# Order of the output stages' halves, and of some sums, loads and weights, in a two-layer encoder kernel

## Chip, core and metric

The kernel runs on one core of a Trainium2 chip. The time is the device time of one execution in microseconds; the time before is a median of 3 runs.

## What is computed

A trunk of two layers over 1024 tokens of 1024 features, with 256 memory tokens, all in float32. Cut from the reference:

```python
for l in range(DEPTH):                                  # 2 layers
    h = rmsnorm(x, norm_gain[l])
    mk, mv = jnp.split(memn @ w_mem_kv[l], 2, axis=-1)
    if l % 2 == 0:
        qa, ka, va, qb, kb, vb, qm, gate = split_cols(h @ w_in_even[e], SPLIT_EVEN)
        # qa, ka: per-head rmsnorm and 2-D rope; ya: global attention, 8 heads
        # yb: window of +-128 tokens with a sink and a bias, 8 heads; ym: attention to memory
        y = jnp.concatenate([ya, yb, ym], axis=-1) * jax.nn.silu(gate)
        x = x + y @ w_out_even[e]
    else:
        qc, kc, vc, qm, gate = split_cols(h @ w_in_odd[o], SPLIT_ODD)
        # yc: attention to 8 x 16 neighbours on the token grid, 16 heads; ym: memory
        y = jnp.concatenate([yc, ym], axis=-1) * jax.nn.silu(gate)
        x = x + y @ w_out_odd[o]
return rmsnorm(x, final_norm_gain)
```

## The kernel before, in words

Every product is taken in three parts for precision: a float32 operand is split into a high part (rounded, `wh`, `H`, `t`) and the rest (`wl`), and TensorE (PE) multiplies high by high, high by low and low by high. ACT makes high parts (L122), DVE or POOL low parts (L155, L1250, L126). Weights come through four buffers: a raw tile `wraw` by SP's DMA queue (L135 in `wload`, L1295 in `out_project`), then `wh` and `wl`. PE's tiles are 128 x 512 in PSUM; `tr`, `sa`, `pv`, `pj`, `x`, `y` and `s` are PSUM tiles by their tags.

The program runs through these stages; the times are of the profiled execution.

- **prep** (to about 120 us) and the entry of **l0**: `project_a` computes norms, values, and keys and queries with rope (its last instruction is the sum `rp`, L869, on POOL) and the keys and values of the memory. `self.loaded` holds back weight loads in `wload` until a given instruction is issued.
- **l0** (to about 650 us): `even` runs global attention in pairs of heads, memory attention, and the windowed attention `window_pair`. Each result is multiplied with its gate by `gated_rows` (L505 to L520: sums on DVE and POOL and stores to DRAM arrays `y_k`). In l0 the weights are split on POOL, both `wh` (L153) and `wl` (L155).
- **out0** (about 645 to 780 us): `out_project`, the output product, by Strassen's scheme in Winograd's form on 2 x 2 blocks: seven products, each over four tiles (banks) of 6 x 128 rows, with weight sums `s1` to `s4` in DRAM made earlier. `y_parts` loads and splits the moving operand of a product (named t1, t2, t3, y22, y21, t4 there; the tile tags in PSUM order are `sa`, `tr`, `pv`, and the SBUF tags are q, k, va, v, H). `weights(i, kind)` loads and splits one bank's weights as two halves of 384 columns, u = 0 and 1. In the trace these are L1302 (matmuls) and L1250, L122 (splits). `plus` adds a bank to its sum (L1311).
- **front** (about 780 to 1035 us): products of layer 1's projection, again by seven products, in an order written out by hand in the string PLAN: `x` and `z` are products (12 matmuls each, L1549), `V` is a step of the values (L410, whose weights `t` are split on ACT and DVE, L402), `.` is a step of the norm, and a digit is that many steps of the operands' differences.
- **l1** (from about 1035 us): `odd` runs memory attention and the neighbourhood attention `near`; PE's order is pinned there to the written order. `near_bias`, `load_q` and `load_v` load what `near` needs; `values_of_two` stores values to `vd` (L421).
- **out1** (from about 1384 us): `out_project` again, with `self.held` a list of instructions that splits must stand behind.

What sets the order elsewhere is a scheduler with priorities: `ahead(kind)` moves an instruction forward by a number of places, and `issue_after(i)` forbids it to stand ahead of `i`. On its own engine and queue every instruction then runs in the order written.

## Time and profile before

| | |
|---|---|
| median of 3 runs | 1504.66 us (1504.38 to 1507.83) |
| the profiled execution's own time | 1509.32 us |
| its span, and clock granted to PE | 1507.5 us, 0.995 |
| PE busy | 1476.3 us (98%) |
| DVE, ACT, POOL busy | 1040.6, 839.5, 635.0 us |
| DMA | 271.90 MB, mean 180 GB/s |

The profile's page gives for each engine the busy time and the number of instructions. Of the 31.2 us in which PE is idle, 1.3 lie at the start, 6.4 behind the last matmul, and 22.4 in gaps of over 0.15 us between. A row such as `PE sa L1302 <- ACT wh L122: 1.8, 1, 1.8` says that PE waited for 1.8 us in all, once, at most 1.8 us, ahead of a matmul of line 1302 into the tile `sa`, and that the wait ended with ACT's instruction of line 122 that wrote `wh`. In a timeline a row starts with start and length in us, and a wait stands at its end in square brackets. In a chain of waits, each piece is what released the next.

### The profile page before, as it was taken

To read this page: it belongs to the slowest core of one execution; us is meant where nothing else is said; L and a number is where in the kernel's file an instruction comes from. 1 tells how busy PE (TensorE), PEld (TensorE's weight loads), DVE (VectorE), ACT (ScalarE), POOL (GpSimd) and SP (SyncE) were. 2 spreads that over 40 slices of the span, in tenths; PEclk is the share of its full clock that TensorE was granted. 3 is DMA by queue.
4 is the path that set the end of the run, shared out by engine and by line. 5 is a ranking of instruction groups with operands and counts; after the bars stand their busy time and mean duration, and the time that the engine had idled before them with its cause. 6 is when DMAs were issued, how large, how long until landed. Compare 5 with 4: busy or idle time off the path is not lost.

```text
span 1507.5 us, 25294 instructions
## 1 busy us (share of the span) xinstructions
PE 1476.3 (98%) x8377; PEld 1269.2 (84%) x8377; DVE 1040.6 (69%) x2121; ACT 839.5 (56%) x1855; POOL 635.0 (42%) x762
## 2 busy tenths in 40 slices
PE   9999999999999999999999999999999999999997
PEld 8897888989888788877879877888988888888886
DVE  5787777677676677677577776654347778788754
ACT  7733665655655456554444444444446777777443
POOL 1224567556765656443440000002325555654355
PEclk9999999999999999999999999999999999999998
DMA  8966244433333424387653343567864677688834
GB/s 286 319 159 185 93 125 165 126 120 123 128 126 135 136 87 138 114 283 257 195 179 106 125 138 135 160 168 256 289 192 158 191 242 218 215 288 308 294 113 138
DMA packets 173859, 271.90 MB, mean 180 GB/s; under 512 B 15648, under 2 KB 96800, under 8 KB 172704
## 3 DMA queue, kind: packets, MB, share of 16 engines
q1 hardware_dynamic: 173296, 270.20, 55.5%
q8 instruction: 66, 1.08, 0.3%
q14 instruction: 65, 0.53, 0.1%
q10 hardware_dynamic: 432, 0.09, 0.0%
HBM read 174.28 MB, written 83.89 MB: 171 GB/s over the span
## 4 chain that ended last, share of the span: by engine, by line
PE 47%; DVE 4%; DMA 3%; issue 1%; POOL 1%; ACT 1%; POOLq 0%; SPq 0%; DVEq 0%; ACTq 0%
PE pj L62 10%; PE x L1549 6%; PE pj L1302 4%; PE sa L1302 4%; PE pv L62 3%; PE y L1549 3%; PE s L62 3%; PE s L1302 3%; PE tr L1302 2%; PE tr L62 2%; PE pv L1549 2%; PE pv L1302 2%; PE pv L410 2%; PE y L410 1%; DMA v<-vt 1%
## 5 line engine op out<-in xcount | busy, mean ns | idle before, releaser
L122 ACT ACTIVATE ph<-tr 128x512 fp32r<-128x512 f32 (+2 forms) x336 | 180.5, 539 | 120.5 <-PE tr L130 79.7
L533 DVE TENSOR_TENSOR pl<-tr,ph 128x512 fp32r<-128x512 f32 (+2 forms) x336 | 205.5, 615 | 52.4 <-ACT ph L122 49.3
L237 PE MATMUL pj<-H,wh 128*128 128x512 f32 x704 | 234.7, 413 | 0.5 <-DVE vt L308 0.2
L153 POOL TENSOR_SCALAR wh<-wraw 128x512 fp32r<-128x512 f32 x48 | 32.0, 666 | 283.6 <-PE x L1549 240.4
L122 ACT ACTIVATE wh<-wraw 128x384 fp32r<-128x384 f32 (+1 forms) x163 | 89.0, 554 | 99.1 <-PE sa L1302 13.5
L237 PE MATMUL pj<-H,wl 128*128 128x512 f32 x352 | 138.9, 395 | 0.0
L237 PEld LDWEIGHTS pj<-H,wh 128*128 128x128 f32 x704 | 119.9, 189 | 18.5 <-POOL wl L155 0.6
L62 PE MATMUL pj<-H,wh 128*128 128x512 f32 x384 | 121.5, 397 | 0.0
L130 PE MATMUL tr<-ident,P 128*128 128x128 f32 x752 | 116.8, 273 | 2.5 <-POOL P L708 1.1
L1101 POOL TENSOR_SCALAR pn<-pn,st 128x384 f32<-128x384 f32 (+1 forms) x128 | 74.9, 586 | 101.3 <-DVE st L1100 64.1
L1250 POOL TENSOR_TENSOR wl<-wraw,wh 128x384 fp32r<-128x384 f32 x56 | 62.7, 1120 | 115.2 <-ACT wh L122 81.5
L130 PEld LDWEIGHTS tr<-ident,P 128*128 128x128 f32 x752 | 89.0, 140 | 12.2 <-DVE pl L533 2.7
L1099 ACT ACTIVATE pn<-pn,st 128x384 f32<-128x384 f32 (+1 forms) x128 | 75.1, 587 | 36.3 <-DVE st L1096 33.9
L1022 ACT ACTIVATE P<-sa,st 128x1024 f32<-128x1024 f32 x64 | 71.5, 1117 | 41.2 <-DVE st L1021 21.6
L1024 POOL TENSOR_SCALAR P<-P,st 128x1024 f32<-128x1024 f32 x64 | 74.1, 1161 | 32.4 <-DVE st L1023 32.4
L62 PE MATMUL s<-k,q 128*128 128x384 f32 (+1 forms) x352 | 86.3, 341 | 0.0
L1021 DVE TENSOR_REDUCE st<-sa 128x1 f32<-128x1024 f32 x64 | 77.6, 1218 | 10.8 <-PE sa L1017 9.2
L237 PEld LDWEIGHTS pj<-H,wl 128*128 128x128 f32 x352 | 66.2, 188 | 15.1
L62 PE MATMUL pj<-H,wl 128*128 128x512 f32 x192 | 75.8, 395 | 0.0
L155 POOL TENSOR_TENSOR wl<-wraw,wh 128x512 fp32r<-128x512 f32 x52 | 68.5, 1318 | 10.2 <-ACT wh L122 7.1
L1250 DVE TENSOR_TENSOR wl<-wraw,wh 128x384 fp32r<-128x384 f32 (+1 forms) x67 | 50.1, 747 | 31.3 <-ACT wh L122 31.0
L62 PEld LDWEIGHTS pj<-H,wh 128*128 128x128 f32 x384 | 66.7, 189 | 5.5
(506 smaller groups left out, 4207.9 us busy)
## 6 DMA issues: line engine op xcount, KB each, us to landing
wraw<-w_o SPq DMA_DIRECT2D x52, 256.0 KB, 3.9
y<-yb SPq DMA_DIRECT2D x24, 512.0 KB, 3.3
wraw<-s SPq DMA_DIRECT2D x64, 192.0 KB, 3.2
wraw<-w_e SPq DMA_DIRECT2D x44, 256.0 KB, 3.2
k<-k SPq DMA_DIRECT2D x42, 256.0 KB, 4.4
s<-bias SPq DMA_DIRECT2D x56, 192.0 KB, 2.0
y<-sg SPq DMA_DIRECT2D x20, 512.0 KB, 3.7
wq<-w_o SPq DMA_DIRECT2D x40, 256.0 KB, 3.6
```

The costliest lines, as they stand in the source:

```text
L62: return lambda *a, **k: self.tc.keep_in_program_order(getattr(self.engine, name)(*a, **k))
L122: return self.nc.scalar.activation(out, in_, AF.Copy, scale=scale)
L130: self.turned = self.fence = self.pe.transpose(o, i, self.ident)
L237: self.pe.matmul(a[:, :n], s[:, kt % UNIT, :], m, start=(kt == 0 and i == 0), stop=(kt == KT - 1 and i == 2))
L533: self.low = nc.vector.tensor_tensor(pl[:, :n], tr[:, :n], ph[:, :n], op=OP.subtract)
L1021: nc.vector.tensor_reduce(st[:, 0:1], s, axis=AX.X, op=OP.max, negate=True)
L1024: self.normal = nc.gpsimd.tensor_scalar(pt, pt, st[:, 2:3], 0.5, op0=OP.mult, op1=OP.mult)
L1099: nc.scalar.activation(o, o, AF.Exp, bias=st[:, 0:1], scale=-1.0, accum_out=st[:, 2:3])
L1101: normal = nc.gpsimd.tensor_scalar(o, o, st[:, 3:4], 0.5, op0=OP.mult, op1=OP.mult)
L1250: engine.tensor_tensor(lf, raw, hf, op=OP.subtract)
L1302: last = nc.tensor.matmul(bank, s[:, k, :], y[3 * u + k][m][:, cols], start=start and u + k + e == 0, stop=u == 1 and k + e == 4, skip_gro ...
L1549: self.last = nc.tensor.matmul(bank, ws[s][:, k, :], b[k][m], start=start and k + i == 0, stop=k == UNIT - 1 and i == 2, skip_group_check= ...
```

## The change

- PLAN: the third `x` product stands ahead of the first `V`.
- `project_a`: the loads of the memory's tokens for their norms, and weight loads behind them, stand behind the tenth weight load instead of behind the last transposition of the memory.
- `wparts`: where POOL makes `wh`, it stands behind the last rope sum.
- `even`: the gated rows of tile 6 are made step by step, one step per pair of blocks of the last window, behind POOL's last scaling there (`later_job`).
- `out_project`: the second and third product run over all four banks with the first half of their depth, then over all four with the second half (`products`), and the first two weights of the second product are loaded ahead of its moving operand.
- `behind_held`: in out1 the first sums, and at the end of `near` the last gated rows, stand behind `self.held`.
- `near_bias`, `load_q`, `load_v`: these loads stand behind the last store of values.

```diff
-PLAN = "x.x.V1V1V2V1V1V1V2V1V1V1V2V1V1V1V2V1x2z2V1V1V2V1V1V1V2V1V1V1V2V1V1V1V2V1x2z2z2z2"
+PLAN = "x.xx.V1V1V2V1V1V1V2V1V1V1V2V1V1V1V2V1x2z2V1V1V2V1V1V1V2V1V1V1V2V1V1V1V2V1z4z2z2"
...
             d = self.nc.sync.dma_start(raw, src)
+        self.raws.append(d)
...
-            nc.gpsimd.tensor_scalar(hf, raw, 1.0, 1.0, op0=OP.mult, op1=OP.mult)
+            with self.tc.issue_after(self.rotated.ins):
+                nc.gpsimd.tensor_scalar(hf, raw, 1.0, 1.0, op0=OP.mult, op1=OP.mult)
...
-                    nc.sync.dma_start(vd[:, :, b + e, :].rearrange("j p n -> p j n"),
+                    self.stored = nc.sync.dma_start(vd[:, :, b + e, :].rearrange("j p n -> p j n"),
...
             for t in range(0, len(todo), 2):
+                self.later_job(normal)
...
-        nc.gpsimd.tensor_tensor(rp, t1, u, op=OP.add)
+        self.rotated = nc.gpsimd.tensor_tensor(rp, t1, u, op=OP.add)
...
         vm = self.st("xv", [128, 2])
+        self.loaded = self.raws[9]
         self.rstd(io["mt"], [0, 1], vm, self.rs_m)
...
-        self.nc.sync.dma_start(bm, self.io["offsets"][h])
+        with self.tc.issue_after(self.stored.ins):
+            self.nc.sync.dma_start(bm, self.io["offsets"][h])
...
-        while self.later_jobs:
-            deque(self.later_jobs.popleft(), 0)
+        with self.behind_held():
+            while self.later_jobs:
+                deque(self.later_jobs.popleft(), 0)
...
+    def behind_held(self):
+
+        with ExitStack() as held:
+            for i in self.held:
+                held.enter_context(self.tc.issue_after(i.ins))
+            yield
...
-        def weights(i, kind):
+        def weights(i, kind, us=(0, 1)):
...
-            for c in cut:
+            for c in (cut[u] for u in us):
...
+        def products(y, banks, kind, start, ready=()):
+            ready = deque(ready)
+            for u in range(2):
+                for i, bank in enumerate(banks):
+                    (h, l), = (ready.popleft(),) if ready else weights(i, kind, (u,))
+                    for k in range(3):
+                        for e, (s, m) in enumerate(((h, 0), (h, 1), (l, 0))):
+                            nc.tensor.matmul(bank, s[:, k, :], y[3 * u + k][m], start=start and u + k + e == 0,
+                                             stop=u == 1 and k + e == 4, skip_group_check=True)
+                    if u:
+                        yield i
...
-            with self.ahead("sink"):
+            with self.behind_held(), self.ahead("sink"):
                 plus(at(c11, i), xb[i])
...
+        ready = [w for i in range(2) for w in weights(i, "s1", (0,))]
         y = self.y_parts(yd, tags["y"][1], "t1")
-        for i in range(4):
-            product(y, yb[i], weights(i, "s1"), True)
+        for i in products(y, yb, "s1", True, ready):
...
         y = self.y_parts(yd, tags["y"][2], "t2")
-        for i in range(4):
-            product(y, xb[i], weights(i, "s2"), False)
+        for i in products(y, xb, "s2", False):
...
-                self.lazily(lambda: self.gate(w, E_G + 6), lambda sg: self.gated_rows(sg, 6, y6, yd))
+                self.later_jobs = deque()
+                self.lazily(lambda: self.gate(w, E_G + 6),
+                            lambda sg: self.later_jobs.append(self.gated_steps(sg, y6, yd, ROWS.index(6))))
...
+        while self.later_jobs:
+            deque(self.later_jobs.popleft(), 0)
         self.gated_rows(sgs[0], 7, y, yd)
...
+    def later_job(self, normal):
+
+        if self.later_jobs:
+            with self.tc.issue_after(normal.ins):
+                if next(self.later_jobs[0], self) is self:
+                    self.later_jobs.popleft()
...
         def load_q(j):
-            return [self.load("q", qd[O_Q + j][i]) for i in range(2)]
+            with tc.issue_after(self.stored.ins):
+                return [self.load("q", qd[O_Q + j][i]) for i in range(2)]
...
         def load_v(j):
-            return self.load("v", vd[j // 2][j % 2], (128, 8, 256)).rearrange("p b (h d) -> p b h d", h=2)
+            with tc.issue_after(self.stored.ins):
+                v = self.load("v", vd[j // 2][j % 2], (128, 8, 256))
+            return v.rearrange("p b (h d) -> p b h d", h=2)
```

What this moves is seen in the order of the instructions on an engine. First POOL at the entry of l0 (about 130 to 148 us): `rp` is the last sum of a rope step, `wh` and `wl` the parts of the first gate weights, `P` the scaling of the first softmax. Before:

```order
L869 TENSOR_TENSOR rp_1734<-rt_323_1716,rt_328_1730 128x512
L153 TENSOR_SCALAR wh_2138<-wraw_2136 128x512
L155 TENSOR_TENSOR wl_2139<-wraw_2136,wh_2138 128x512
L869 TENSOR_TENSOR rp_1926<-rt_364_1908,rt_369_1922 128x512
L153 TENSOR_SCALAR wh_2144<-wraw_2142 128x512
L155 TENSOR_TENSOR wl_2145<-wraw_2142,wh_2144 128x512
L869 TENSOR_TENSOR rp_2008<-rt_375_1990,rt_380_2004 128x512
L153 TENSOR_SCALAR wh_2417<-wraw_2415 128x512
L155 TENSOR_TENSOR wl_2418<-wraw_2415,wh_2417 128x512
```

Now, the same piece:

```order
L874 TENSOR_TENSOR rp_1734<-rt_323_1716,rt_328_1730 128x512
L874 TENSOR_TENSOR rp_1926<-rt_364_1908,rt_369_1922 128x512
L874 TENSOR_TENSOR rp_2008<-rt_375_1990,rt_380_2004 128x512
L157 TENSOR_SCALAR wh_2138<-wraw_2136 128x512
L157 TENSOR_SCALAR wh_2144<-wraw_2142 128x512
L159 TENSOR_TENSOR wl_2139<-wraw_2136,wh_2138 128x512
L159 TENSOR_TENSOR wl_2145<-wraw_2142,wh_2144 128x512
L157 TENSOR_SCALAR wh_2417<-wraw_2415 128x512
L157 TENSOR_SCALAR wh_2423<-wraw_2421 128x512
L159 TENSOR_TENSOR wl_2418<-wraw_2415,wh_2417 128x512
```

All weights stand behind the last `rp`, and two `wh` ahead of two `wl`.

Second ACT at the entry of out0 (about 664 to 680 us): `wh` are the halves of the weights, `ph` and `bt` belong to the last attention, `q`, `k` and `va` are parts of the operand y22 of the fifth product (`y_parts`), loaded ahead. Before:

```order
L122 ACTIVATE wh_8263<-wraw_8261 128x384
L122 ACTIVATE ph_8120<-tr_8117 128x256
L122 ACTIVATE wh_8278<-wraw_8276 128x384
L122 ACTIVATE wh_8295<-wraw_8293 128x384
L122 ACTIVATE q_8708<-q_8708 128x512
L122 ACTIVATE wh_8310<-wraw_8308 128x384
L122 ACTIVATE q_8709<-q_8709 128x512
L122 ACTIVATE k_8710<-k_8710 128x512
L122 ACTIVATE wh_8327<-wraw_8325 128x384
```

Now:

```order
L124 ACTIVATE wh_8241<-wraw_8239 128x384
L124 ACTIVATE wh_8247<-wraw_8245 128x384
L124 ACTIVATE ph_8121<-tr_8118 128x256
L124 ACTIVATE wh_8294<-wraw_8292 128x384
L124 ACTIVATE wh_8309<-wraw_8307 128x384
L124 ACTIVATE q_8709<-q_8709 128x512
L124 ACTIVATE bt_8127<-pv_8041 64x512
L124 ACTIVATE q_8710<-q_8710 128x512
L124 ACTIVATE k_8711<-k_8711 128x512
L124 ACTIVATE k_8712<-k_8712 128x512
L124 ACTIVATE wh_8324<-wraw_8322 128x384
```

The four first halves of the second product (wh_8241, wh_8247, wh_8294, wh_8309) stand ahead of the first `q`; before, a `wh` stood behind each of the first `q` and `k`.

Third SP's queue at the entry of front (about 774 to 783 us): `wraw` of 128x512 are weights of the x products, those of 128x2x256 the weights `t` of the values, `wq` the operands of the weights' own sums. Before:

```order
L135 DMA wraw_9392<-w_o 128x512
L135 DMA wraw_9413<-w_o 128x2x256
L1767 DMA x_6_115<-yb_8151 128x512
L135 DMA wraw_9417<-w_o 128x2x256
L1767 DMA x_7_116<-yb_8151 128x512
L1588 DMA wq_9319<-w_o 128x512
```

Now:

```order
L137 DMA wraw_9393<-w_o 128x512
L137 DMA wraw_9412<-w_o 128x512
L1792 DMA x_6_115<-yb_8152 128x512
L137 DMA wraw_9433<-w_o 128x2x256
L1792 DMA x_7_116<-yb_8152 128x512
L1613 DMA wq_9320<-w_o 128x512
```

One more weight of an x product is ahead of the `wq` loads, and one load of `t` less. On PE the 12 matmuls of the third x product now stand between those of the second and the transpositions of `rq_y` (`tr` L130, now L132) ahead of the first matmul of the values.

More of the change, by code (lines that the diff above doesn't have):

```diff
@@ L84, in __init__ @@
         self.pe, self.ready, self.due = self.nc.tensor, {}, 0
-        self.loaded = None
+        self.loaded = self.rotated = None
+        self.raws = []
+        self.later_jobs = ()
     def ahead(self, kind):
@@ L420, in values_of_two @@
                     self.vec.tensor_tensor(o[:, :, :, 1, :], src, o[:, :, :, 0, :], op=OP.subtract)
-                    nc.sync.dma_start(vd[:, :, b + e, :].rearrange("j p n -> p j n"),
-                                      o.bitcast(F32).rearrange("p j h e d -> p j (h e d)"))
+                    self.stored = nc.sync.dma_start(vd[:, :, b + e, :].rearrange("j p n -> p j n"),
+                                                    o.bitcast(F32).rearrange("p j h e d -> p j (h e d)"))
             yield 3072
@@ L1191, in halves @@
         return tiles
+    @contextmanager
+    def behind_held(self):
[3 more added lines that the diff above has]
+            yield
     def y_parts(self, yd, tags, kind):
@@ L1207, in y_parts @@
                 nc.sync.dma_start(raw, src[kind])
-                with ExitStack() as held:
-                    for i in self.held:
-                        held.enter_context(self.tc.issue_after(i.ins))
+                with self.behind_held():
                     self.split(hi, lo, raw)
```

## Prediction

> **What bounds the kernel now.** I read the page's first part first, then what TensorE (PE) waits for, then the 25-us stretches around each wait, then the chain of waits there.
>
> ```profile
> PE 1476.3 (98%) x8377; PEld 1269.2 (84%) x8377; DVE 1040.6 (69%) x2121; ACT 839.5 (56%) x1855; POOL 635.0 (42%) x762
> ```
>
> PE is busy for 1476.3 us of a span of 1507.5 us, and no other engine passes 69%. In the order of its instructions PE has the same matmuls before and after the change, so the change can only move the 31.2 us in which PE stands, and what the clock costs. The list of PE's waits (us in total, times, longest) names where it stands:
>
> ```profile
> PE pv L62 <- DVE pl L533: 4.1, 8, 1.1
> ...
> PE sa L1302 <- ACT wh L122: 1.8, 1, 1.8
> PE y L410 <- ACT t L122: 1.6, 1, 1.6
> PE tr L130 <- POOL rp L869: 1.4, 2, 1.1
> ...
> PE tr L130 <- POOL P L708: 1.1, 3, 0.7
> ...
> PE tr L552 <- ACT wh L122: 1.1, 2, 0.7
> ...
> PE sa L1016 <- DVE q L126: 0.8, 1, 0.8
> ```
>
> All these groups but the first consist of one to three waits, so each is a place, not a habit of a loop; each part of the change lies at one of them. Then the stretches: start:end, length, busy us of PE, PEld, DVE, ACT, POOL, granted clock, DMA share, GB/s.
>
> ```profile
> 25.00:50.00 25.00, 23.44 (x167) 21.20 (x167) 12.07 (x25) 19.45 (x46) 9.03 (x7) 1.00 0.94 315
> 675.00:700.00 25.00, 23.13 (x92) 18.39 (x93) 16.00 (x23) 11.25 (x21) 10.39 (x9) 0.93 0.74 242
> 775.00:800.00 25.00, 21.71 (x120) 18.58 (x121) 15.83 (x33) 13.49 (x25) 5.84 (x4) 0.93 0.70 232
> ```
>
> Two stretches have a clock of 0.93, and both hold a wait: each loses about 0.07 x 25 = 1.7 us of full clock on top of the idle time. The Trainium skill, "TensorE: Matmul & The Clock Gate" (What's actually happening), has the clock halve after an idle window of about 3.4 us; the longest wait here is 1.8 us, so by that rule the two drops would not be there, and the trace disagrees with it in two places. By the rule the clock term below would be nothing, and the sum 1.7 us smaller in size.
>
> **The change part by part.** I sum against the profiled execution, 1509.32 us: its span of 1507.5 and 1.8 around it. It is 4.66 us above the median of 1504.66; I take differences over to the median. Signs: minus is time gained.
>
> *Loads of prep (raws[9]).* SP's issues, start and length:
>
> ```profile
> 24.91 2.99 SPq L785 DMA_DIRECT2D xt<-mt x3
> 28.26 1.68 SPq L135 DMA_DIRECT2D wraw<-w_mem x3
> ```
>
> The three mt loads and their 2.99 us stand ahead of weights for which PE waits (tr L552 behind wh, 1.1, and small ones after it, 1.56 us in all by PE's rows at 34.8 to 38.6). Now two of the weights go ahead of the mt loads. The queue is 0.94 busy there, so bytes only change places: what comes later are mt and w_a, whose users stand later in PE's order by 1.4 us. I take -1.0; ends -1.6 (all waits gone) and +2 (the mt loads, 2.99 us, late in their turn by two thirds).
>
> *POOL's weight splits behind the last rope sum.* POOL, then DVE, in the last two rope steps:
>
> ```profile
> 133.34 1.34 POOL L155 TENSOR_TENSOR wl<-wraw,wh 128x512 fp32r<-128x512 f32 x1
> ...
> 140.92 1.26 POOL L869 TENSOR_TENSOR rp<-rt,rt 128x512 f32<-128x512 f32 x1 [2.56 <-DVE rt L866]
> ...
> 147.65 1.12 POOL L1024 TENSOR_SCALAR P<-P,st 128x1024 f32<-128x1024 f32 x1 [1.55 <-DVE st L1023]
> ```
>
> ```profile
> 132.68 2.28 DVE L866 TENSOR_TENSOR rt<-rqn,c_sinq 128x256 f32<-128x256 f32 x2
> ...
> 137.13 1.25 DVE L766 SCALAR_TENSOR_TENSOR iq_t<-iq_t,rss 128x8 f32<-128x8 f32 x1
> ...
> 140.02 0.75 DVE L866 TENSOR_TENSOR rt<-rqn,c_sinq 128x256 f32<-128x256 f32 x2
> ```
>
> PE waits 1.09 us for the second rp and 0.76 us for q behind it. The same pair of DVE instructions takes 2.28 us beside POOL's wl and 0.75 us without it: 1.5 us of the chain to rp, and L766, with 8 columns, takes 1.25 us beside the next wl, about 1 too much. Without these, the last rp is there near 138, not at 142.2, and the first wait is gone; the second needs a split on DVE that also stands behind ACT, so I count 0.4 of its 0.76. Sum -1.5. What is late next: four wh and four wl (4 x 0.62 by POOL's rows and 4 x 1.3, together 7.7 us) now run after rp, to about 147, ahead of P, which starts at 147.65: cover of 0.6 us. Ends: -1.9 (both waits gone), +1 (rp not earlier, P pushed by about 2, half of it seen by PE).
>
> *Second product by halves, two weights ahead (out0).* The chain of waits, start and length:
>
> ```profile
> 668.81 6.00 DMA q<-y
> ...
> 674.83 0.63 ACT q L122
> ...
> 675.98 0.51 ACT wh L122
> ```
>
> ACT has the split of q (part of the operand y22 of the fifth product, loaded from y, 6.00 us) ahead of the weight wh that PE needs next, so the weight waits for a transfer that it has nothing to do with: 1.8 + 0.33 us of PE, and the clock drop right after. In the changed order all four first-half weights stand ahead of q, and PE has 36 matmuls (8.4 us) of first halves to do before any second half. Both waits go, -2.1, and with them the drop, -1.7. Earlier, tr waits 0.73 behind POOL:
>
> ```profile
> 645.57 3.07 POOL L708 TENSOR_SCALAR P<-P,st 128x384 f32<-128x384 f32 x4
> ```
>
> That P is queued behind three sums of gate 6 (L516, L517, L519, 4.3 us by POOL's rows from 641.34). By steps after each block's normal they come behind P: I count 0.3 of the 0.73, since the sums must still be run. New: the last part of t2's operand comes back through y_11. Its chain starts at the last eviction and ends with the last split:
>
> ```profile
> 677.03 0.59 ACT L122 ACTIVATE bt<-pv 64x512 f32<-64x512 f32 x1
> ```
>
> ```profile
> 701.18 1.31 DVE L126 TENSOR_TENSOR H<-H 128x512 fp32r<-128x512 f32 x2 [2.95 <-ACT H L122]
> ```
>
> That is 25.5 us. Before, 101 matmuls of 512 columns and 4 us of waits stood in that time; now 114 matmuls, 26.4 us at 0.2315 each (2.78 us for 12, quoted below), and no waits: a cover of about 1 us, with six transfers in the chain. So I add a wait of +0.8; ends 0 and +3 (the chain lengthened by half of the 6.00 us transfer). Sum for this place: -2.1 - 0.3 - 1.7 + 0.8 = -3.3; ends -4.5 and +3.
>
> *PLAN: the third x product ahead of the values.*
>
> ```profile
> 783.07 7.06 DMA wraw<-w_o
> ```
>
> ```profile
> 787.14 0.65 PE L130 MATMUL tr<-ident,rq_y 128*128 128x128 f32 x4 [0.66 <-DVE rq_y L256]
> 787.55 1.68 PE L410 MATMUL y<-t,H 128*128 128x256 f32 x12
> 790.84 0.39 PE L410 MATMUL y<-t,H 128*128 128x256 f32 x1 [1.61 <-ACT t L122]
> ```
>
> ```profile
> 815.34 2.78 PE x L1549 x12
> ```
>
> PE waits 0.66 for rq_y, then 1.61, 0.34 and 0.28 for the t tiles, whose loads stand behind four wq loads. An x product of 12 matmuls takes 2.78 us. Put between them it covers rq_y's wait whole. But its own weight load is put ahead as well: by SP's order one t load of two slips behind the wq loads. I work out PE at tr from 789.1, y for one tile to 790.4, then the second t at 791.5, the third at 792.2, the fourth at 793.6 (DVE has four 0.7-us splits in line), the first 24 y matmuls done at about 794.3 instead of 793.4, with 2.78 us of work more behind it: -1.9. About 1.6 us of idle stay close together, so I count the second clock drop as staying: 0. Ends -4.6 (both go) and +1 (t two splits later than I have it).
>
> *The loads of l1 behind the last store.* SP and PE:
>
> ```profile
> 1110.46 1.02 SPq L421 DMA_DIRECT2D v<-vt x2
> ...
> 1127.03 0.51 SPq L361 DMA_DIRECT2D k<-k x1
> ```
>
> ```profile
> 1134.73 0.40 PE L62 MATMUL s<-k,q 128*128 128x256 f32 x2
> ```
>
> Four q (0.5 MB each), two bm (0.33) and two v (1.05) make 4.9 MB, now issued after 1111.5, with 1 MB of y behind them. At the 315 GB/s of the stretch 25:50 they land in 18.7 us, at 1130.2, and the copies of k just after; the first score needs them at 1134.73: cover of some 3 us. What is gained is one wait of 0.37 for a store late in the queue. I take -0.2; ends -0.4 and +3 (the cover used up once over).
>
> *y's sums behind at near's end (behind_held, the draining).* The chain:
>
> ```profile
> 1381.99 0.59 DVE H L1311
> ...
> 1382.60 0.51 DVE yb L473
> ...
> 1383.22 0.56 DVE pl L533
> ```
>
> Two sums stand ahead of the pl for which PE waits 1.15 us (the longest of the first group of waits). In the new order pl goes first; the two sums, 1.3 us, feed transfers with 2.5 us of cover. -1.1; ends -1.3 and 0. The same edits in out1 find no wait of PE to remove.
>
> **Sum:** -1.0 - 1.5 - 3.3 - 1.9 - 0.2 - 1.1 = -9.0 us. 1509.32 becomes 1500.3 in a profiled execution, and the median 1504.66 becomes **1495.7**. A change below 0.3% (4.5 us) could not be told from none here.
>
> **The rivals.**
> (1) *The clock drops stay or were not in the median.* That the profile is 4.66 us above the median could be the two drops (3.4 us) that other executions don't have; and if t2's operand also comes 2 us late instead of 0.8, the sum is -9.0 + 1.7 + 1.2 = -6.1: 1498.6. For it: the drop depends on where idle falls. Against: the wait ahead of the first drop goes as a whole.
> (2) *The halves do nothing.* PE's old order already runs some first halves ahead of q's tiles, and if ACT gets the weights' loads no sooner, the place keeps its waits; then only the other terms count, -5.7; if POOL's new order likewise gives nothing (the rope sums held up by the last split of q instead), -4.2: 1500.5, not to be told from none. For it: the second halves still need v, loaded from the same y behind it, and the later q still has ACT stand. Against: 8.4 us of first halves stand between.
> (3) *Slower: the bunched loads of l1 come too late.* 5.9 MB and 1 MB of k copies must land from 1111.5 to 1134.7, 23.2 us: 297 GB/s. This decides. At 315 GB/s nothing happens; at 242 (the stretch 675:700, not full) they take 28.5 us, a wait of 5.3. To end slower by over 0.3%, the wait must eat 9.0 and 4.5: 36.7 us, 188 GB/s, and the time would be about 1510. For it: one queue carries stores, loads and copies, and PE's order is pinned there, so that PE can't go round the wait. Against: q and bm, needed first, are issued first.
>
> **How the numbers follow.** The forecast has 0.57 (own range 1490.6 to 1499.5), rival 1 0.18, rival 2 0.13, rival 3, as any wait of this kind that the bunching makes, 0.12. Faster by over 0.3%: 0.57 + 0.18 = 0.75; within 0.3%: 0.13; slower: 0.12. The lower end is the sum of the good ends, -1.6 - 1.9 - 4.5 - 4.6 - 0.4 - 1.3 = -14.3, at 1490.4. The upper end takes in rivals 1 and 2, and on top of rival 2's -4.2 the bad ends of POOL's place (+1) and of l1's loads (+3.2 against the -0.2): 0 in all, 1504.7, rounded to 1505.
>
> **What would show it.** Right: PE's list of waits without sa L1302 behind wh and without tr behind rp; a clock of 1.00 in the stretch that was 675:700; pl ahead of H at near's end; PE's idle below 24 us. Wrong: a product that waits for H around the t2 stage; y L410 with a wait above 2 us; s behind k or bm at the start of near; P L1024 late near 148. It would be wrong as a whole if PE's busy time itself moved, for the sum holds it still.

## The result, and the profile after

The changed kernel takes 1508.7 us (median of 14 runs, 1504.62 to 1511.04), the kernel before 1507.26 us in its own 14 runs (1503.03 to 1512.81): a ratio of 1.0006 with a 95% interval of 0.9992 to 1.0020. So there is no difference that can be measured; 9 us less were forecast. The profiled execution of the changed kernel took 1506.25 us, 3.07 us less than the profiled one of before, while its median is 1.4 us higher: one execution each does not settle 3 us in a kernel whose own runs lie 10 us apart.

The page's first part after the change:

```profile
PE 1475.8 (98%) x8377; PEld 1269.3 (84%) x8377; DVE 1033.2 (69%) x2122; ACT 840.6 (56%) x1855; POOL 633.7 (42%) x762
```

PE's busy time held still, as assumed. The list of PE's waits after the change (total, times, longest):

```profile
PE pv L62 <- DVE pl L537: 2.6, 6, 0.8
PE pj L1328 <- DVE wl L1264: 2.4, 1, 2.4
PE tr L132 <- DVE rq_y L62: 1.9, 2, 1.4
PE tr L132 <- POOL rp L874: 1.8, 1, 1.8
PE pj L1316 <- DVE wl L1264: 1.5, 1, 1.5
...
PE tr L1328 <- DVE wl L1264: 1.0, 1, 1.0
PE sa L1022 <- DVE q L128: 1.0, 1, 1.0
...
PE y L414 <- DVE t L406: 0.3, 1, 0.3
...
PE tr L132 <- POOL P L712: 0.2, 1, 0.2
```

The named waits of before are gone or small: those of sa behind wh (1.8) and of y behind t on ACT (1.6) are gone, tr behind P is 0.2 instead of 1.1, and the longest wait of pv behind pl is 0.8 instead of 1.1. In their places stand three waits for a weight's low part on DVE (2.4, 1.5 and 1.0) and a longer one for rp (1.8). They lie at the same stages: 2.4 and 1.0 at out0's entry (691 and 681 us), 1.5 at out1's (1422 us), 1.8 in prep (60 us). All gaps over 0.15 us add up to 19.8 us against 22.4. The stretches with a lowered clock moved too:

```profile
50.00:75.00 25.00, 23.04 (x158) 21.43 (x156) 18.64 (x51) 18.62 (x49) 4.30 (x5) 0.93 0.93 303
675.00:700.00 25.00, 21.52 (x84) 15.94 (x83) 18.42 (x26) 12.81 (x25) 9.00 (x8) 0.93 0.87 295
775.00:800.00 25.00, 24.21 (x141) 20.50 (x140) 17.65 (x37) 13.06 (x24) 5.85 (x4) 1.00 0.75 238
```

The front stage (775 to 800) is mended in both ways: PE 24.21 busy instead of 21.71, and the clock full. (How much of that is due to the change is a question for the other runs, further down.) Out0's stretch still has its 0.93 and PE is busy less there than before (21.52, was 23.13); prep has a drop that it hadn't.

**What happens at out0's entry.** POOL, SP and DVE of the changed kernel, as timelines (start, length):

```profile
658.24 3.47 POOL L712 TENSOR_SCALAR P<-P,st 128x384 f32<-128x384 f32 x4 [4.01 <-DVE st L707]
661.68 1.60 POOL L497 TENSOR_TENSOR yb<-sg,yb 128x512 f32<-128x512 f32 x1
```

```profile
663.31 0.33 SPq L498 DMA_DIRECT2D y<-yb  x1
...
670.47 0.35 SPq L1223 DMA_DIRECT2D q<-y  x1
```

```profile
690.52 0.68 DVE L1337 TENSOR_TENSOR P<-P,tr 128x512 f32<-128x512 f32 x1
691.12 0.90 DVE L128 TENSOR_TENSOR q<-q 128x512 fp32r<-128x512 f32 x1
691.94 0.67 DVE L1337 TENSOR_TENSOR P<-P,pv 128x512 f32<-128x512 f32 x1
692.53 0.55 DVE L1264 TENSOR_TENSOR wl<-wraw,wh 128x384 fp32r<-128x384 f32 x1
```

Read from the top: the last sum of tile 6's gated rows now stands behind the last block's P on POOL and runs at 661.68; before, the same sum (L519) ran at 644.30. Its store is issued at 663.31 (before 646.04), and SP issues nothing between 658.4 and that moment. The first load of y22 behind it, q, is issued at 670.47 instead of 667.91. Further down, a product of out0 waits 2.4 us for wl, which DVE makes only after two sums of the product that has just ended and a split of q for a later one.

### The profile page after: what moved, and what is told of

It reads as the page before. It is cut to its first block, busy times and chain, and to the rows that moved or that the text cites. A ratio compares the mean times of both kernels' runs of the same rounds, so it can differ in the third digit from the quotient of the medians.

```text
span 1504.5 us, 25295 instructions
## 1 busy us (share of the span) xinstructions
PE 1475.8 (98%) x8377; PEld 1269.3 (84%) x8377; DVE 1033.2 (69%) x2122; ACT 840.6 (56%) x1855; POOL 633.7 (42%) x762
## 4 chain that ended last, share of the span: by engine, by line
PE 82%; DMA 6%; DVE 6%; issue 2%; POOL 2%; ACT 2%; SPq 1%; POOLq 0%; DVEq 0%; ACTq 0%
PE pj L241 15%; PE pj L62 11%; PE x L1574 6%; PE tr L132 5%; PE pv L1055 4%; PE y L1574 4%; PE pv L62 3%; PE s L62 3%; PE pj L1316 3%; PE tr L62 2%; PE pv L1574 2%; PE sa L1316 2%; PE s L1316 2%; PE sa L1022 2%; PE sa L1023 2%
## 5 line engine op out<-in xcount | busy, mean ns | idle before, releaser
L132 PE MATMUL tr<-ident,P 128*128 128x128 f32 x752 | 115.8, 273 | 0.8 <-DVE pl L537 0.6
L132 PEld LDWEIGHTS tr<-ident,P 128*128 128x128 f32 x752 | 89.0, 140 | 9.5 <-DVE pl L537 2.1
L1028 ACT ACTIVATE P<-sa,st 128x1024 f32<-128x1024 f32 x64 | 71.5, 1117 | 40.0 <-DVE st L1027 21.3
L840 PE MATMUL pj<-ah,H 128*128 128x256 f32 x384 | 71.3, 283 | 0.1
```

The source lines that it names most:

```text
L132: self.turned = self.fence = self.pe.transpose(o, i, self.ident)
L1028: nc.scalar.activation(pt, s, AF.Exp, bias=st[:, 0:1], accum_out=st[:, 1:2])
```

## The experiments

What was open: is the net zero made of gains and losses of about equal size (theory), or were most of the gains not there (rival)? Each part was therefore run alone, and several were undone. A name with b_ is the kernel before with the named part added, a name with a_ the changed kernel with the named part taken out. Each of these kernels ran 7 to 12 times beside 30 to 35 runs of the kernel before on the same chip (the changed kernel itself 14 times beside 14). Ratios are to the kernel before; microseconds are the ratio less 1, times 1506.5, which is about the median of the kernel before.

| kernel | ratio (95%) | us against before |
|---|---|---|
| changed kernel | 1.0006 (0.9992 to 1.0020) | +0.9 |
| before + PLAN (b_plan) | 0.9978 (0.9963 to 0.9993) | -3.3 |
| before + halves (b_halves) | 0.9993 (0.9981 to 1.0005) | -1.1 |
| before + rope sums ahead (b_rotated) | 0.9993 (0.9980 to 1.0006) | -1.1 |
| before + loads behind the last store (b_stored) | 0.9992 (0.9979 to 1.0004) | -1.2 |
| before + prep's line (b_raws) | 1.0002 (0.9989 to 1.0015) | +0.3 |
| before + held sums (b_held) | 1.0017 (1.0002 to 1.0032) | +2.6 |
| before + tile 6 by steps (b_gate6) | 1.0036 (1.0019 to 1.0054) | +5.4 |
| changed - prep's line (a_noraws) | 0.9999 (0.9981 to 1.0017) | -0.2 |
| changed - halves (a_nohalves) | 0.9997 (0.9984 to 1.0011) | -0.5 |
| changed - both (a_noraws_nohalves) | 1.0001 (0.9985 to 1.0016) | +0.2 |
| changed - steps of tile 6 (a_nogate6) | 0.9985 (0.9971 to 0.9999) | -2.3 |
| changed - steps, prep's line, held sums (a_best) | 0.9969 (0.9956 to 0.9983) | -4.7 |
| b_plan + y22's splits later (b_plan_y22) | 0.9992 (0.9979 to 1.0005) | -1.2 |
| a_noraws + y22's splits later (a_noraws_y22) | 1.0015 (1.0002 to 1.0027) | +2.3 |
| b_gate6, last step earlier (b_gate6m) | 1.0023 (1.0006 to 1.0040) | +3.5 |
| a_best + such steps (a_best_gate6m) | 0.9987 (0.9975 to 0.9999) | -2.0 |

**The seven parts alone, added:** -3.3 - 1.1 - 1.1 - 1.2 + 0.3 + 2.6 + 5.4 = +1.6, against +0.9 (-1.2 to +3.0) measured together. By these values the zero is a gain of about 6.7 and a loss of about 8.3. Only for PLAN, the held sums and the steps does the interval leave out 1, and the sum of seven such measurements is itself uncertain by some 5 to 6 us (an estimate from the seven intervals, taken as independent). That the parts add up is therefore not contradicted, but not shown closely. In one place the traces show that they don't: the wait for wl at 1421 to 1427 us (1.4 to 1.9 us long) stands in the four kernels that have both the halves and the held sums, and in none that has only one of them or neither.

### First: the two suspects of the trace, undone, and PLAN alone

The first suspects were the prep line and the halves, whose waits the trace shows.

```diff
-        self.loaded = self.raws[9]
```

> The changed kernel without the line that ties prep's loads to the tenth weight load. Theory (the parts that gain are eaten by waits that other parts create): the wait of 1.76 us of tr behind rp near 60 us falls back to about 0.3, the small waits of wh near 38 us (0.6) come back, and the clock of 0.93 in the stretch 50 to 75 is 1.00: 1 to 3 us faster than the changed kernel. Rival (the single profile misleads, and the parts neither gain nor lose in most executions): same as the changed kernel within 0.5 us.

Measured: the wait near 60 is 0.85 instead of 1.76, of the small waits near 38 one of 0.23 comes back, and the clock of 50 to 75 is 1.00. The time is 0.9999 of before, within the changed kernel's interval; the theory's 1 to 3 us are not shown. Out0 waited even longer in this execution (0.58, 1.02 and 3.16 us).

```diff
-        ready = [w for i in range(2) for w in weights(i, "s1", (0,))]
...
-        for i in products(y, yb, "s1", True, ready):
+        for i in range(4):
+            product(y, yb[i], weights(i, "s1"), True)
...
-        for i in products(y, xb, "s2", False):
+        for i in range(4):
+            product(y, xb[i], weights(i, "s2"), False)
```

> The changed kernel with the second and third output product bank by bank as before. Theory (the halves put several sums and splits of one moment on DVE ahead of the next product's weights): the waits near 681 (1.0), 691 (2.38) and 1422 us (1.49) go; those of before at 675 us (1.8 and 0.33) may come back; 1 to 4 us faster than the changed kernel. Rival (the halves gain as forecast, and the loss lies elsewhere): 2 to 4 us slower than the changed kernel.

Measured: 0.9997, which is 1.4 us under the changed kernel: inside the theory's 1 to 4, and not clear of nothing. The waits at 681, 691 and 1422 go, but one of 3.84 us comes at 674, where before had 1.8: more than either side expected. Something other than the halves made out0's entry worse, and bank by bank shows it as one long wait.

> Both undone. Theory: the two effects add up, 3 to 6 us faster than the changed kernel, and clear of the kernel before by 0.2 to 0.4%. Rival: same as the changed kernel within 1 us.

Measured: 1.0001, with a wait of 3.56 us at 674. That is 0.7 us under the changed kernel, where the theory had 3 to 6: these two parts aren't where the gain went.

```diff
-PLAN = "x.x.V1...x2z2z2z2"
+PLAN = "x.xx.V1...z4z2z2"
```

> The kernel before with the new PLAN alone. Theory: the waits of 0.66, 1.61, 0.34 and 0.28 us near 786 to 793 us shrink to about 0.4 in all and the clock drop there goes, so 3 to 5 us faster than before, 0.2 to 0.35%. Rival (the gain of the front stage is eaten later, by l1's DMA or its own weights): within 1 us of before.

Measured: 0.9978 (0.9963 to 0.9993), 3.3 us. The stretch 775 to 800 of this kernel:

```profile
775.00:800.00 25.00, 23.79 (x135) 19.80 (x134) 16.75 (x36) 12.79 (x22) 5.84 (x4) 1.00 0.74 235
```

PE works 2.1 us more there than in the profile of before, and at full clock. The rival falls: a gain is there at the end (1.1 to 5.6 us), so it is not eaten later. But the profile of before is no fair measure of this place. The seven other profiled kernels with the old PLAN (b_halves, b_gate6, b_gate6m, b_held, b_raws, b_rotated, b_stored) all have a clock of 1.00 in 775 to 800, and their waits for rq_y and the t tiles add up to 1.0 to 1.6 us, where before has 2.9 (its wait of 1.61 stands in none of them). With the new PLAN it is 0 to 0.9 us in ten profiles. So the traces show a gain of some 0.9 us in waits, and what else the 3.3 us hold is not seen in them.

### Second: out0's entry

```diff
+        ready = [w for i in range(2) for w in weights(i, "s1", (0,))]
...
-        for i in range(4):
-            product(y, yb[i], weights(i, "s1"), True)
+        for i in products(y, yb, "s1", True, ready):
...
-        for i in range(4):
-            product(y, xb[i], weights(i, "s2"), False)
+        for i in products(y, xb, "s2", False):
...
```

> The kernel before with the second and third output product by halves alone. Theory (the halves move the wait from ACT to DVE, where the splits of operand y22 and four sums stand ahead of the next weights' low parts): the waits of 1.8 and 0.33 us near 675 us go, waits of 1 to 3 us near 681, 691 and 1425 us come, so 1 us faster to 3 us slower than before. Rival (the halves gain as forecast, another part of the change takes it back): 3 to 4 us faster than before.

Measured: 0.9993, 1.1 us, not clear of nothing. The wait for wh at 675 is gone and waits of 0.86 and 1.42 us stand at 690 and 693. The clock of 675 to 700 is 1.00 in this execution. The halves alone about break even: the theory's range holds, the rival's 3 to 4 us are just outside the interval (-2.9 to +0.8). The two new waits have different causes. The 0.86 is for a weight's low part; the 1.42 is for a sum, P, that must empty the bank `sa` before PE may write it again:

```profile
691.19 0.50 PE L1314 MATMUL pj<-H,wl 128*128 128x512 f32 x1 [0.86 <-DVE wl L1250]
...
694.50 0.70 PE L1314 MATMUL sa<-H,wh 128*128 128x512 f32 x2 [1.42 <-DVE P L1323]
```

```diff
-                self.later_jobs = deque()
-                self.lazily(lambda: self.gate(w, E_G + 6),
-                            lambda sg: self.later_jobs.append(self.gated_steps(sg, y6, yd, ROWS.index(6))))
+                self.lazily(lambda: self.gate(w, E_G + 6), lambda sg: self.gated_rows(sg, 6, y6, yd))
```

> The changed kernel with the gated rows of tile 6 in one piece as before. Theory (the steps delay the last store of these rows, and with it SP's loads of y22): q's load is issued about 2 us sooner than the changed kernel's, the waits near 681 and 691 shrink by 1 to 2 us, the wait of 0.73 us of tr behind P near 646 comes back; 0 to 2 us faster than the changed kernel. Rival (the steps cost nothing later): 0.7 us slower.

Measured: 0.9985 (0.9971 to 0.9999), some 3 us better than the changed kernel (the two intervals just overlap), and the first version with the halves whose out0 is calm: 0.33 and 0.82 us are all that is left near 690. The load of q is issued at 668.29, 2.2 us sooner, as the theory has it. The wait behind P near 646 comes back as 0.31 and 0.42.

The same steps added to the kernel before, alone:

> The kernel before with the gated rows of tile 6 made by steps alone. Theory (the steps push the last sum of these rows, and with it a store in SP's queue and the loads behind it, back by some 17 us): the wait of 0.73 to 0.8 us of tr behind P near 646 goes, the wait of sa for wh near 675 grows from 1.8 to 3.5 us and more, and the time is 1 to 3 us above before. Rival (the steps are harmless, and the loss in the changed kernel needs the halves): 0.7 us faster, the wait near 675 as before.

Measured: 1.0036 (1.0019 to 1.0054): 5.4 us slower, more than the theory's 1 to 3. A row of its list of waits, its stretch, and POOL's and SP's rows:

```profile
PE sa L1304 <- ACT wh L123: 3.7, 1, 3.7
```

```profile
675.00:700.00 25.00, 21.28 (x84) 16.86 (x83) 13.12 (x20) 9.44 (x18) 8.17 (x7) 0.86 0.73 249
```

```profile
664.86 1.28 POOL L494 TENSOR_TENSOR yb<-sg,yb 128x512 f32<-128x512 f32 x1
```

```profile
666.17 0.33 SPq L495 DMA_DIRECT2D y<-yb  x1
```

The wait for wh grew from 1.8 to 3.7, and the clock fell to 0.86 over 25 us, 3.5 us of full clock instead of 1.7. The late sum and the late store are there. Against that only the wait of 0.73 behind P is gone: against the profile of before, 1.6 + 1.8 - 0.7 = 2.7 us of the 5.4 can be read off this trace. The clock's share is larger over all runs: their mean granted clock is 0.9946 (7 runs) against 0.9968 (30 runs of before), and 0.0022 of 1507 us is 3.3 us. With this estimate in place of the 1.8 it is 4.2 of the 5.4.

**Two tests of the mechanism, both against my theory.** The first: is y22's split, ahead of the weights, what holds the line? Its splits were put behind the last weight of the second product on ACT.

```diff
+        self.acted = self.copy(hf, raw)
...
+        t1 = self.acted
         y = self.y_parts(yd, tags["y"][2], "t2")
...
-        y = self.y_parts(yd, tags["y"][4], "y22")
+        with nullcontext() if last else self.tc.issue_after(t1.ins):
+            y = self.y_parts(yd, tags["y"][4], "y22")
```

> The kernel before with the new PLAN, and in out0 the splits of operand y22 on ACT behind the last weight of the second product. Theory (the head of line is y22's split, not the order of the halves): the waits of 1.8 and 0.33 us near 675 us go without halves, and 2 to 4 us more are gained than by PLAN alone, 5 to 7 us against before, 0.35 to 0.5%. Rival (the weights are late by their own DMA): a wait of 1 us and more for wh stays near 675 us and the time is that of PLAN alone, 3 us under before.

> The changed kernel without prep's line, and y22's splits on ACT behind the last weight of the second product. Theory: the wait of 1 us near 682 goes and that of 2.4 to 3.2 us near 692 shrinks below 1 us, with the clock drops there; 3 to 5 us faster than the same without this line (a_noraws). Rival (the four sums of the end of t1 alone hold DVE): the wait near 692 stays at 2 us and more.

Measured: 0.9992 and 1.0015; with this edit the first is not better than PLAN alone, the second no better than a_noraws. The waits aimed at do go (1.8 near 675 in the one, 1.0 near 682 in the other), but one of 2.15 us comes at 686 in the first, and in the second the longest of all at 689:

```profile
PE pj L1327 <- DVE wl L1263: 5.0, 1, 5.0
```

In both a later weight's low part is what PE now waits for, on POOL (L1250) in the one and on DVE in the other: with the splits moved, the wait moved too.

The second: is it the late store? The last two steps were made one, so that the last sum comes ahead of the last P.

```diff
-lambda sg: self.later_jobs.append(self.gated_steps(sg, y6, yd, ROWS.index(6))))
+lambda sg: self.later_jobs.append(self.merged(self.gated_steps(sg, y6, yd, ROWS.index(6)), 5)))
...
+    def merged(self, steps, n):
+        for _ in range(n):
+            next(steps)
+            yield
+        deque(steps, 0)
```

> The kernel before with tile 6's gated rows by steps, but the last step made together with the one before it, so that the last sum stands ahead of the last block's scaling on POOL. Theory (the last sum's store holds SP's queue, and with it the weights and y22 behind it): the store y<-yb is issued near 648 instead of 666 us, the wait of sa for wh near 675 falls from 3.7 to below 2, and the 5.4 us of the steps shrink to 1 or less against before. Rival (the steps as such cost, by shifting loads and splits): the wait stays above 3 us and the time 4 us and more above before.

Measured: 1.0023 (1.0006 to 1.0040). The store is early now, and the waits are there all the same:

```profile
646.78 1.12 SPq L495 DMA_DIRECT2D y<-yb  x1
```

```profile
PE sa L1304 <- ACT wh L123: 2.1, 1, 2.1
...
PE sa L1304 <- DVE wl L1252: 1.1, 1, 1.1
...
PE tr L1304 <- DVE pl L534: 0.9, 1, 0.9
```

Together 4.2 us, and the clock of the stretch is 0.86 again. By the ratios some 2 us of the steps' 5.4 belong to the store, but the two kernels' intervals overlap, so even these are not shown. The other 3.5 stay with the steps as such.

What else the steps move is seen on POOL. Before, and here:

```profile
645.57 3.07 POOL L708 TENSOR_SCALAR P<-P,st 128x384 f32<-128x384 f32 x4
...
653.09 4.26 POOL L708 TENSOR_SCALAR P<-P,st 128x384 f32<-128x384 f32 x4
```

```profile
657.65 3.38 POOL L709 TENSOR_SCALAR P<-P,st 128x384 f32<-128x384 f32 x4 [4.02 <-DVE st L704]
661.00 1.98 POOL L1252 TENSOR_TENSOR wl<-wraw,wh 128x384 fp32r<-128x384 f32 x2
```

The last four scalings of P start 21 us behind the four before them (657.65, after 636.23), where before has 7.5 us. So it is in all kernels of this case: 21.3 to 22.4 us in the eight with steps, 7.5 to 8.6 in the ten without. The sums of tile 6 are done by 646.7 here and don't hold this P, and still it is late, with the weights' low parts behind it. SP waits 4.1 us for one of them (before 2.9) until it can load the next weights.

> The changed kernel without prep's line and without out1's held sums, with the steps of tile 6 mended in the same way. Theory: as good as the same kernel without the steps (a_best), or 0.5 us better, since the wait of 0.8 us of tr behind P near 648 goes: 4 to 6 us faster than before. Rival: at least 2 us slower than that kernel.

Measured: 0.9987 against 0.9969 without any steps: 2.7 us lost again by mended steps, as the rival has it (the two intervals just overlap). Its clock in 675 to 700 is 1.00, and the mean over its runs (0.9977) is not below that of a_best (0.9974): what is lost here is not lost by the clock.

Over all kernels, PE's waits of over 0.25 us between 660 and 700 us add up as follows. With tile 6 by steps: 3.4 (changed), 4.8 (a_noraws), 3.8 (a_nohalves), 3.6 (both), 5.0 (a_noraws_y22), 3.7 (b_gate6), 4.2 (b_gate6m), 3.9 (a_best_gate6m). In one piece: 2.1 (before), 2.2 (b_plan), 2.3 (b_halves), 3.0 (b_plan_y22), 1.2 (a_nogate6), 1.8 (a_best), 1.8 (b_held), 1.3 (b_raws), 2.0 (b_rotated), 1.8 (b_stored). The two groups do not overlap, whatever else was changed. That the steps make out0's entry worse by some 2 us of wait is shown, and that the last P is late with them; that this P and not another reordered instruction makes the waits is not.

### Third: the parts at the edges

```diff
-        while self.later_jobs:
-            deque(self.later_jobs.popleft(), 0)
+        with self.behind_held():
+            while self.later_jobs:
+                deque(self.later_jobs.popleft(), 0)
...
-            with self.ahead("sink"):
+            with self.behind_held(), self.ahead("sink"):
                 plus(at(c11, i), xb[i])
```

> The kernel before with the sums of out1's entry behind the held instructions alone. Theory (the same sums are late for the next product's operand): the wait of 1.15 us of pv near 1383 goes, a wait of 1.2 us or more comes near 1389 to 1425, and the time is that of before within 1 us. Rival (gain as forecast): 1.1 us faster, no new wait at out1's entry.

Measured: 1.0017 (1.0002 to 1.0032), slower, if anything. The wait of 1.15 of pv is gone, and this row of PE's timeline stands in its place:

```profile
1390.22 0.50 PE L1311 MATMUL tr<-k,wl 128*128 128x512 f32 x1 [1.24 <-DVE wl L1259]
```

DVE has the same run of splits (four k, two q, five H, k) ahead of that wl in both kernels. Before, PE came later by the wait that it had just had; now it meets the next one. That explains a gain of nothing, not a loss of 2.6; the rest isn't seen in this trace, and with an interval from 0.3 to 4.8 it may be small.

```diff
+        self.raws.append(d)
...
+        self.loaded = self.raws[9]
```

> The kernel before with prep's line alone. Theory (bytes change places in a full queue): the small waits behind wh near 38 us shrink by some 0.6 us, the wait of tr behind rp near 60 us grows from 0.3 to about 1.7; 1 to 2.5 us slower than before. Rival (gain as forecast): 1 us faster, the wait near 60 us below 0.5.

Measured: 1.0002 (0.9989 to 1.0015). The wait for rp near 60 is 1.88 us, as the theory has it, and the small ones from 35 to 39 are less (1.05 in all instead of 1.56), but the time is that of before. In the four profiled kernels with this line the wait for rp is 1.76 to 1.88 us; in the others it is anything up to 1.65.

```diff
...
+            with self.tc.issue_after(self.rotated.ins):
+                nc.gpsimd.tensor_scalar(hf, raw, 1.0, 1.0, op0=OP.mult, op1=OP.mult)
```

> The kernel before with POOL's weights behind the last rope sum alone. Theory: the wait of 1.1 to 1.4 us of tr behind rp near 142 goes, that of sa for q near 145 stays at about 1.0: 1 us faster than before, not clear of its interval. Rival (the weights split late delay the first softmax): a wait behind P near 148 us and no gain.

Measured: 0.9993. There is no wait behind the last rp, that of sa for q is 0.99 instead of 0.76, and nothing waits for P near 148. The sum forecast (-1.5) is within the interval, and so is nothing. The wait that goes is not in every execution either: of the nine profiled kernels without the part, before and three others have it (1.09 to 1.42 us), and five have 0.24 or none.

```diff
...
+        with self.tc.issue_after(self.stored.ins):
+            self.nc.sync.dma_start(bm, self.io["offsets"][h])
...
```

> The kernel before with l1's loads behind the last store alone. Theory: the wait of pv near 1085 to 1090 (0.4 to 1.7 us from run to run) goes, waits of some 0.7 to 1.4 us in all come near 1131 to 1136 at near's first scores: within 1 us of before. Rival (the bunched loads come far too late): a wait above 3 us near 1131.

Measured: 0.9992. The wait of pv near 1085 (0.37 in the profile of before, 0.49 to 2.34 in seven of the other eight kernels without this part) is gone, and one of 0.71 at 1135 is the longest at near's start: the slow rival of the prediction falls.

### Fourth: the parts that gain, together

```diff
-        self.loaded = self.raws[9]
...
-        with self.behind_held():
-            while self.later_jobs:
-                deque(self.later_jobs.popleft(), 0)
+        while self.later_jobs:
+            deque(self.later_jobs.popleft(), 0)
...
-            with self.behind_held(), self.ahead("sink"):
+            with self.ahead("sink"):
```

(and tile 6 in one piece as in a_nogate6)

> The changed kernel without three of its parts: prep's line, the steps of tile 6, and the held sums of out1. PLAN, the halves, the rope sums ahead of the weights and the loads behind the last store stay. Theory (the three parts cost, the four gain): no wait above 1.5 us near 675 to 695 or near 1425, and 4 to 7 us faster than before, 0.25 to 0.45%. Rival (the parts' effects don't add up, since each shift of the schedule makes waits of its own): 2 us faster or less.

Measured: 0.9969 (0.9956 to 0.9983), 4.7 us by the ratio (the medians are 1501.43 and 1506.61): the fastest of all kernels tried. Its stretch at out0's entry:

```profile
675.00:700.00 25.00, 23.23 (x97) 17.67 (x96) 16.52 (x25) 12.40 (x25) 9.25 (x8) 1.00 0.87 288
```

Full clock, with 1.17 and 0.59 us of waits. The four parts alone sum to -6.7, at the edge of this interval (-6.6 to -2.6).

## Why the prediction was wrong

The forecast summed six terms to -9.0; the parts alone measure +1.6. Two things failed: the steps of tile 6 were priced by their sums alone, and waits and clock drops were counted that belong to the one execution that was profiled. By its steps:

- **Loads of prep, forecast -1.0, measured +0.3 (b_raws).** "Bytes only change places" was right, but "what comes later are mt and w_a" leaves out the loads of x. The chain of waits of the changed kernel runs through them (the ninth lands at 55.9 us, before at 52.2),

```profile
45.21 5.04 DMA xt<-xt
...
51.09 4.85 DMA xt<-xt
```

and ends at rp, for which PE waits 1.76 us. The end of +2 had about this size, by the mt loads; the sum had nothing for it.
- **POOL's weights behind rp, forecast -1.5, measured -1.1 (-3.0 to +0.9).** Not contradicted: no wait for rp is left and P isn't pushed. But the wait for q is not 0.4 shorter, it is 0.23 longer, and the wait for rp is missing in five of nine profiles without this part.
- **Halves and tile 6 at out0's entry, forecast -3.3, measured -1.1 and +5.4.** This is the step that failed. It says: "By steps after each block's normal they come behind P: I count 0.3 of the 0.73, since the sums must still be run." I counted the three sums on POOL and not what else the steps move: the store at their end in SP's queue, the last P itself, and the order in which the scheduler puts weights and splits around them. That is a miss of 5.7 us of the 10 between forecast and result. The halves' term was mis-sized too: both named waits went as said, but "a wait of +0.8" should have been 2.3 (0.86 and 1.42 in b_halves). It was not for H, whose chain through y_11 came in time, but for DVE, where splits for later products stand ahead of the next weight's low part and of the sum that empties a bank. And "with them the drop, -1.7" took a gain that five of six profiles don't have (below). Without it, and with 2.3 in place of 0.8, the halves' share is +0.2, within the interval of what was measured (-2.9 to +0.8).
- **PLAN, forecast -1.9, measured -3.3 (1.1 to 5.6).** The right way, and rq_y's wait is covered, as said; of the 1.6 us of idle that I left at the t tiles 0.34 are left (ahead of 794.12 in the changed kernel). But the size is not explained: the wait of 1.61 and the clock drop there are in the profile of before alone, and against the seven other profiles with the old PLAN only some 0.9 us of wait goes. The term stands within the interval; that is no proof of its parts.
- **The loads of l1, forecast -0.2, measured -1.2 (-3.2 to +0.6).** The size is not told from nothing, and rival 3 falls: no wait above 0.71 us at near's start (1.04 is the longest in any kernel with this part).
- **The held sums, forecast -1.1, measured +2.6 (0.3 to 4.8).** The step "pl goes first; the two sums, 1.3 us, feed transfers with 2.5 us of cover" looked at who waits for the sums. It should have asked what is late next for PE: wl, by 1.24 us. The prediction also says that "the same edits in out1 find no wait of PE to remove"; together with the halves they make one there, the 1.4 to 1.9 us near 1422.

**The profile summed against was not a typical execution.** The forecast took its terms from one execution of 1509.32 us with a mean granted clock of 0.995. Of the 135 runs of the kernel before that stand beside the experiments, 7 have 0.995 (1510.7 us on average), 42 have 0.996, 45 have 0.997 and 41 have 0.998 (1505.0 us). In out0's stretch (675 to 700), b_held, b_plan, b_raws, b_rotated and b_stored still have the order of before and a wait of 1.05 to 1.79 us for wh, and all five have a clock of 1.00 there. So the drop of -1.7 stands in one of six profiles with that order, and most of it was not there to be won. PE's busy time, which the sum holds still, is 1471.6 us in one profile (b_raws) and 1478.9 in another (a_noraws), a span of 7.3 us.

The two first-named rivals each had a piece of it. Rival 2 (the place keeps its waits) is near the time, but for another reason than the halves doing nothing. Rival 1 says that the two drops could be what "other executions don't have", and that is what the other profiles show; its -6.1 was still far off. (The drop in out0 of the changed kernel is a new one, at 694, behind its new wait of 2.38.) None had a part that costs 5 us. The range ended at 1505.0; the medians are 1507.26 before and 1508.7 after, where the 3 runs shown gave 1504.66, so 2.6 us of the miss in microseconds are the level of the runs themselves. With the ratio applied to 1504.66 the time would be 1505.6, still above the range.

## What to carry to other kernels

When work is put off in small steps, follow every instruction of a step to its own queue, its store above all, and compare the order on the engines that are behind it; the sums themselves were the cheap part. Where PE waits for operands that pass one in-order engine, taking away one wait shows the next in the same line: price the second before counting the first. Before a wait or a clock drop of one profile is counted as gain, ask whether other executions have it; the mean clock of each run already tells. And a change of several parts with a net of nothing is worth taking apart: here four parts of it together gain 0.31%, and with the other three the gain is gone.

## What the runs showed of the hardware

- One kernel's runs lie further apart than expected: 35 runs of the kernel before, on one chip, went from 1500.39 to 1514.88 us. The 3 runs at hand (3.5 us apart) made it look better resolved than it is; 0.3% needs a dozen runs each.
- The clock falls to 0.50 for some us at a time (in the profile of before from 677.4 to 680.6, in b_gate6 0.51 over 680.8 to 687.4), and the 0.93 and 0.86 above are means over 25 us.
- The lowered clock does not follow from one gap's length alone. Waits of 1.8 and 0.33 us near 675 came with 0.93 in the profile of before; 1.79 and 0.36 at the same place came with 1.00 in b_plan; 3.7 us (b_gate6) and 2.1, 1.1 and 0.9 (b_gate6m) with 0.86. The Trainium skill, "TensorE: Matmul & The Clock Gate" (What's actually happening), has the window run free of the program, which fits one wait being charged in one execution and not in the next; its idle window of about 3.4 us is longer than most single waits here that a lowered clock followed; only those of 3.56 (a_noraws_nohalves), 3.72 (b_gate6), 3.84 (a_nohalves) and 4.97 us (a_noraws_y22) are longer.
